# Sixty instead of forty-four seven-product quads in a two-layer encoder's MLPs, with residual additions by accumulating DMA

## The chip, the core and the metric

The kernel runs on one core of one Trainium2 chip. The metric is the device time of one execution in microseconds. The core's engines are TensorE (PE; its weight loads are listed as PEld), VectorE (DVE), ScalarE (ACT), GpSimd (POOL) and SyncE (SP, which here only issues DMAs). Each engine works through its own queue in order.

## The reference

256 tokens of width 2048 pass through two layers. Layer 0 mixes tokens with a convolution module, layer 1 with latent attention; each is followed by an MLP of width 8192, whose two products are most of the work. Everything is float32.

```python
def sq_relu_mlp(h, w1, w2):
    return jnp.square(jax.nn.relu(h @ w1)) @ w2

# for each layer
x = x + mixer(rms_norm(x, norm_mixer_g[i]))
x = x + sq_relu_mlp(rms_norm(x, norm_mlp_g[i]), mlp_w1[i], mlp_w2[i])
# at the end
return rms_norm(x, final_norm_g)
```

## The kernel before

The residual `xs` stays on chip: 128 partitions, two token tiles (t = 0, 1), 2048 columns, which are four blocks of 512 (n = 0 to 3). A float32 product is made of three products of rounded parts: `mm3` adds hi x hi, lo x hi and hi x lo. The weights stream in by DMA from SP's queue, 1 MB at a time, into `raw` (three buffers). ACT makes the `hi` part (L168, for mixed quads L489) and DVE the `lo` part by a subtraction (L172, for mixed quads L490); `hi` and `lo` have six buffers each (`WB`).

**The MLP** runs in two halves of the 8192 columns; (layer, half) names one of the four half-layers. The up product of a half goes through eight groups g of 512 columns (L615, L616). After a group's last matmul DVE and ACT evacuate it (L634 to L643): square of the positive part, then hi and lo for the next product. The down product follows. It takes two column blocks at a time, a pair, and walks over the half's 32 k-tiles in 16 **quads** of 2 k-tiles x 2 blocks x 2 token tiles.

**Plain and mixed quads.** A plain quad is 8 `mm3`, so 24 matmuls of 128x512. A mixed quad computes the same 2x2 block product with seven multiplications instead of eight: 21 matmuls. For this it needs sums of the four weight blocks, made by DVE in `raw` (L497, L498, L499) before their hi and lo parts, and sums of the inputs, made in the evacuation of its group (`mixed_inputs`). The table `MIXED` says which groups of each half-layer are mixed; each is two mixed quads in each of two column pairs.

**The sums.** `Sums` holds the eight PSUM banks of a pair: four `e[t][c]`, into which plain quads go straight, and four `u`, which only the mixed quads feed and from which three of the four outputs need combinations. `join` makes these after the last mixed quad and adds them to `xs`: one ACT copy and eight DVE operations (L568 to L575). At the pair's end `add` (L376) adds the `e` banks to `xs` with four DVE operations.

**The order** is that of the program's text on each engine. In a pair the quads alternate, mixed ahead of plain, until the mixed ones are used up. In the second pair of a second half, `product_A` takes the place of the plain quads: it goes through the plain groups with one block of 24 matmuls each for n = 2 (4 k-tiles x 2 token tiles), with mixed quads between, and then through n = 3.

**The two ends.** In layer 0's last half the finished residual must be turned (columns to partitions) for the next mixer. Blocks 0 to 2 are turned by DVE: `turn_block` issues 48 STREAM_TRANSPOSE (L322), spread by `turns_on` between the quads of the last column pair, and ACT and DVE then make hi and lo parts. Block 3 is turned by `to_T` with TensorE (L265). In layer 1's last half ACT sums the squares of each finished block (L399) and DVE multiplies it by the final gain (L1769).

The profile's names: `sh`, `sl` are input parts of mixed groups, `gh`, `gl` of plain ones.

Of the kernel before, what the change touches and what calls it, by code (L numbers as in the profile page):

```python
# [21 lines left out]
T = 2  # L22
# [13 lines left out]
HALVES = 2  # L36
PAD_CONST = 24
PAD_SMALL = 48
# [39 lines left out]
def trunk_kernel(  # L78
# [324 lines left out]
    def product_A(  # L403
# [14 lines left out]
        for n in blocks:  # L418
# [54 lines left out]
        while due:  # L473
            prepare(due.pop(0))

    def turns_on(due, prepare, n=4):

        if due and not steps:
            prepare(due.pop(0))
        step(n)  # L480

# [41 lines left out]
    class Sums:  # L523
# [36 lines left out]

        def join(self, pool):

            u1, u6, u7, u5 = self.u
            x = lambda t, c: xs[:, t, (self.n + c) * NB : (self.n + c + 1) * NB]
            a, b = (pool.tile([P, 2, S], F32, tag="v", name=nm("v"), bufs=2).rearrange("p a n -> p (a n)") for _ in range(2))
            tt = nc.vector.tensor_tensor
# [3 lines left out]
            tt(b, u7, a, op=ALU.add)  # L570
            tt(a, u5, a, op=ALU.add)
            tt(x(1, 0), b, x(1, 0), op=ALU.add)
            tt(b, u5, b, op=ALU.add)
            tt(x(0, 1), a, x(0, 1), op=ALU.add)
            tt(x(1, 1), b, x(1, 1), op=ALU.add)  # L575

    def mlp(layer, ssq, next_gain, finish=None, before=None, beside=None):

        with ExitStack() as cx:
# [3 lines left out]
            nssq = None  # L583
            turned = None if next_gain is None else mp.tile([P, NB // P, S], F32, name=nm("turned"))
            r2_row = mp.tile([P, S], F32, name=nm("r2_row"))
            repool(f"mlp{layer}", acc=8)

            def scales():
# [8 lines left out]
            for hf in range(HALVES):  # L597
# [4 lines left out]
                for g in range(ng):  # L602
# [20 lines left out]
                    if g in mixed or len(mixed) < N_MIXED and g == plain[-1]:  # L623
                        shape = [P, 2, 7, P] if g in mixed else [P, 4, S]
                        gs[g] = [mp.tile(shape, F32R, tag=f"s{c}", name=nm(f"s{c}"), bufs=N_MIXED) for c in "hl"]
                    else:
                        gs[g] = [mp.tile([P, 4, S], F32R, tag=f"g{c}", name=nm(f"g{c}"), bufs=ng - N_MIXED) for c in "hl"]
                    gh, gl = gs[g]
                    for b2 in range(2):
                        v = mp.tile([P, 2, S], F32, tag="v", name=nm("v"), bufs=2)  # L630
                        for b in range(2):
# [11 lines left out]
                        nc.vector.tensor_tensor(gl[:, bs, :], v, gh[:, bs, :].bitcast(F32), op=ALU.subtract)  # L643
                nssq, add, prepare = residual_stage(
                    last, next_gain, None, turned, () if turned is None else range(NNB - 1)
                )
                w, k_lo = mlp_w2[layer], hf * nkh
# [9 lines left out]
                for n in range(0, NNB - 2 * last, 2):  # L657
                    sums = Sums(n)
                    ks = [4 * g + 2 * b for g in plain for b in range(2)]
                    for i, k in enumerate(ks):  # L660
                        if i < len(ms):
                            mixed_quad(sums, i)
                            turns_on(due, prepare)
                        if i == len(ks) - 2:
                            sums.join(mp)
                        sums.plain(w, k_lo + k, hi, lo, k, i == len(ks) - 1)
                        turns_on(due, prepare)
                    for c in range(2):
                        for t in range(T):
                            add(n + c, [sums.e[i][c] for i in range(T)], t)  # L670
                        if last:
                            due.append(n + c)
                if last:
# [3 lines left out]
                    def between(n, u, due):  # L677
                        if n == n2 and u < len(plain) - 1:
                            lo_i, hi_i = (len(ms) * i // (len(plain) - 1) for i in (u, u + 1))
                            for i in range(lo_i, hi_i):  # L680
                                mixed_quad(sums, i)
                                turns_on(due, prepare)
                        if n == n2 and u == len(plain) - 1:
                            sums.join(mp)

                    product_A(
                        w, k_lo, nkh, hi, lo, add, prepare, range(n2, NNB), due,
# [8 lines left out]
    with ExitStack() as cx:  # L696
# [3 lines left out]
        NW = W * KC // 4  # L700
        w_dw = const.tile([P, W * KC], F32, name="w_dw")

# [543 lines left out]
    def rotary_tables(pool):  # L1246

        place = pool.tile([P, 2, S], F32, tag="v", name=nm("v"), bufs=2).rearrange("p a n -> p (a n)")
        at = [0]
# [512 lines left out]

    with tc.tile_pool(name="fin", bufs=1, reuse_waits="tile") as fp:
        gf = fp.tile([P, D], F32, name="gf")
        nc.scalar.dma_start(gf, final_norm_g.rearrange("(a n) -> a n", a=1).partition_broadcast(P))

        def gained(t, n):
            sl = slice(n * NB, (n + 1) * NB)
            nc.vector.tensor_tensor(xs[:, t, sl], xs[:, t, sl], gf[:, sl], op=ALU.mult)  # L1769

        def finish(ssq, t):
# [18 lines left out]
            for i, (c0, c1) in enumerate(zip(cuts, cuts[1:])):  # L1790
                ob = xs[:, t, c0:c1]
                if c1 == D:
                    nc.vector.scalar_tensor_tensor(
                        out=ob, in0=ob, scalar=y, in1=gf[:, c0:c1], op0=ALU.mult, op1=ALU.mult
                    )
# [24 lines left out]

        mlp(1, ssq, None, finish, before)

# [25 lines left out]
```

## Time and profile before

| | us |
|---|---|
| median of three timed runs | 1955.56 |
| lowest and highest | 1955.26, 1955.60 |
| profiled execution, its own time | 1955.42 |
| profiled span | 1953.6 |
| PE busy | 1932.2 |
| DVE busy | 1547.1 |
| ACT busy | 1058.6 |
| POOL busy | 220.5 |

A row of a group reads: line, engine, operation, output <- input, shapes, count | busy us, mean ns of one | idle us just before them, and what ended it. A row of waits reads: engine, line, what it waited for, us in total, how often, the longest. In a timeline a row begins with its start and its duration in us, "x2" is two instructions in a row, and a bracket at the end gives the idle time before it. In a table of windows each row gives the window, its length, and each engine's busy time; then the granted clock, the DMA engines' busy share and their GB/s. The last number of a DMA row is the time in us from issue to landing. A matmul's busy time overlaps with the next one's.

The down products of the four half-layers, as windows in the trace (first matmul of the pair to that of the next): (0,0) 477.85 to 560.82 and 560.82 to 643.78; (0,1) 821.29 to 905.63 and 905.63 to 996.52; (1,0) 1435.41 to 1518.39 and 1518.39 to 1601.35; (1,1) 1778.86 to 1861.84 and 1861.84 to 1944.00, after which the output is finished.

### The profile page before, as it was taken

The numbers are of one execution on the slowest core, as the hardware profiler recorded it, in microseconds if no ns is written. First come the engines' busy times: TensorE is split into PE (matmuls) and PEld (weight loads), VectorE is DVE, ScalarE is ACT, GpSimd is POOL, SyncE is SP. The second block draws the span as 40 slices with busy tenths as digits, with TensorE's granted clock in tenths as the row PEclk, the third lists the DMA queues.
The fourth block names the chain that finished last, engine by engine and source line by source line (L and its number), as shares of the span: only waits on it lengthen the run. The fifth ranks groups of instructions, "written<-read, shape, count | busy, mean of one in ns | idle before, by whom it ended". The sixth has DMA issues, their size and how long they took to land. (4 is left out here: it accounts for less than half of the span.)

```text
span 1953.6 us, 28331 instructions
## 1 busy us (share of the span) xinstructions
PE 1932.2 (99%) x10835; PEld 1691.2 (87%) x10835; DVE 1547.1 (79%) x2400; ACT 1058.6 (54%) x1568; POOL 220.5 (11%) x172
## 2 busy tenths in 40 slices
PE   8999999999999999999999999999999999999998
PEld 8999888888888888888789998888888888888886
DVE  7999988877988676787966665876788876778896
ACT  5667755554645454454556665555555545455554
POOL 6999100000000000000001310000000000000000
PEclk9999999999999999999999999999999999999999
DMA  7765556664657666564565445566656566664754
GB/s 231 209 192 175 169 180 212 194 187 159 225 191 231 191 185 188 169 231 157 172 193 173 120 144 180 173 223 189 192 171 217 193 222 190 193 193 160 237 168 147
DMA packets 216746, 367.62 MB, mean 188 GB/s; under 512 B 15513, under 2 KB 90529, under 8 KB 216353
## 3 DMA queue, kind: packets, MB, share of 16 engines
q1 hardware_dynamic: 215280, 363.28, 58.7%
q10 hardware_dynamic: 1328, 2.52, 0.4%
q8 instruction: 85, 1.39, 0.3%
q14 instruction: 53, 0.43, 0.1%
HBM read 363.68 MB, written 2.10 MB: 187 GB/s over the span
## 5 line engine op out<-in xcount | busy, mean ns | idle before, releaser
L172 DVE TENSOR_TENSOR lo<-raw,hi 128x1024 fp32r<-128x1024 f32 (+2 forms) x543 | 647.9, 1205 | 294.7 <-ACT hi L168 290.8
L168 ACT ACTIVATE hi<-raw 128x1024 fp32r<-128x1024 f32 (+2 forms) x608 | 622.8, 1040 | 462.6 <-PE acc L615 238.7
L615 PE MATMUL acc<-xt,hi 128*128 128x512 f32 x2048 | 710.5, 390 | 0.0
L616 PE MATMUL acc<-xt,lo 128*128 128x256 f32 x2048 | 577.5, 282 | 0.0
L615 PEld LDWEIGHTS acc<-xt,hi 128*128 128x128 f32 x2048 | 384.4, 188 | 80.6
L616 PEld LDWEIGHTS acc<-xt,lo 128*128 128x128 f32 x2048 | 387.1, 189 | 0.2
L489 ACT ACTIVATE hi<-raw 128x1024 fp32r<-128x1024 f32 (+1 forms) x176 | 164.0, 949 | 179.8 <-DVE raw L497 70.1
L203 PE MATMUL acc<-lo,gh 128*128 128x512 f32 (+1 forms) x644 | 250.2, 388 | 1.1 <-DVE lo L172 0.9
L201 PE MATMUL acc<-hi,gh 128*128 128x512 f32 (+1 forms) x644 | 249.7, 388 | 0.0
L202 PE MATMUL acc<-hi,gl 128*128 128x512 f32 (+1 forms) x644 | 249.7, 388 | 0.0
L490 DVE TENSOR_TENSOR lo<-raw,hi 128x1024 fp32r<-128x1024 f32 (+1 forms) x176 | 188.5, 1087 | 34.2 <-ACT hi L489 30.6
L761 PE MATMUL acc<-xt,hi 128*128 128x256 f32 x1024 | 180.1, 281 | 0.3 <-ACT b L1043 0.2
L848 DVE SCALAR_TENSOR_TENSOR sum<-ub,w_dw,sum 128x256 f32<-128x256 f32 x409 | 164.2, 480 | 3.5 <-ACT sum L818 3.0
L203 PE MATMUL acc<-lo,sh 128*128 128x512 f32 x404 | 157.8, 391 | 2.8 <-DVE lo L490 2.6
L201 PE MATMUL acc<-hi,sh 128*128 128x512 f32 x404 | 157.4, 390 | 0.0
L172 POOL TENSOR_TENSOR lo<-raw,hi 128x1024 fp32r<-128x1024 f32 x65 | 154.9, 2408 | 17.3 <-ACT hi L168 17.3
L761 PEld LDWEIGHTS acc<-xt,hi 128*128 128x128 f32 x1024 | 154.6, 188 | 1.1 <-ACT xt L1027 0.6
L203 PEld LDWEIGHTS acc<-lo,gh 128*128 128x128 f32 x644 | 120.9, 188 | 27.5 <-DVE lo L172 2.7
L201 PEld LDWEIGHTS acc<-hi,gh 128*128 128x128 f32 x644 | 120.9, 188 | 24.8
L202 PEld LDWEIGHTS acc<-hi,gl 128*128 128x128 f32 x644 | 120.9, 188 | 24.7
L761 PE MATMUL acc<-xt,lo 128*128 128x256 f32 x512 | 139.2, 279 | 0.0
L202 PE MATMUL acc<-hi,sl 128*128 128x512 f32 x340 | 132.4, 389 | 0.0
(310 smaller groups left out, 2359.5 us busy)
## 6 DMA issues: line engine op xcount, KB each, us to landing
raw<-in_mlp_w SPq DMA_DIRECT2D x256, 1024.0 KB, 5.4
raw<-in_conv_w_pw SPq DMA_DIRECT2D x62, 512.0 KB, 5.1
raw<-in_conv_w_pw SPq DMA_DIRECT2D x16, 1024.0 KB, 5.1
raw<-in_mla_w_o SPq DMA_DIRECT2D x16, 1024.0 KB, 5.6
raw<-in_mla_w_kv_up SPq DMA_DIRECT2D x8, 1024.0 KB, 5.5
raw<-in_mla_w_in SPq DMA_DIRECT2D x8, 576.0 KB, 3.7
raw<-in_mla_w_in SPq DMA_DIRECT2D x4, 1024.0 KB
raw<-in_mla_w_q_up SPq DMA_DIRECT2D x16, 256.0 KB, 3.3
```

The source lines that it names most:

```text
L168: nc.scalar.activation(hi, raw[:, js, :], AF.Copy)
L172: eng.tensor_tensor(lo, raw, hi.bitcast(F32), op=ALU.subtract)
L201: nc.tensor.matmul(ps, sh, mh, start=start, stop=False)
L202: nc.tensor.matmul(ps, sl, mh, start=False, stop=False)
L203: nc.tensor.matmul(ps, sh, ml, start=False, stop=stop)
L489: nc.scalar.activation(hi, src, AF.Copy)
L490: nc.vector.tensor_tensor(lo, src, hi.bitcast(F32), op=ALU.subtract)
L615: nc.tensor.matmul(ps[b], wh[:, bs], xhl(k), start=k == 0, stop=False)
L616: nc.tensor.matmul(ps[b][:, :S], wl[:, bs], xh(k), start=False, stop=k == KC - 1)
L761: nc.tensor.matmul(pss[c][b][:, :S], w[i][:, bs], (xh, xl)[j](k), start=k == i + j == 0, stop=end and k == k0 + nk - 1 and (i, j) == terms ...
L848: nc.vector.scalar_tensor_tensor(out=out, in0=ubs[c][:, w : w + S], scalar=tap(c, w), in1=base, op0=ALU.mult, op1=ALU.add)
```

## The change

Four things are changed.

1. `MIXED` grows from 11 to 15 groups: 60 mixed quads instead of 44, four groups in each half-layer but (0,1), which has three. The order in a pair follows a rule with `TAIL`: for eight mixed (m) and eight plain (p) quads it is m m p m p m p m m p m p m p p p. In (0,1) it is m p m p m p p m p m p m p p p p. In the second pair of a second half `between` is now called ahead of the first block too; with G for a block of 24 matmuls, (0,1) runs m G m G m G m G m m G and (1,1) m m G four times.
2. `join` makes its combinations in four tiles (`v`, four buffers instead of two), one ACT copy and four DVE operations, and POOL issues four accumulating DMAs (`put`, 256 KB each, SBUF to SBUF) that add them to `xs`. `close` takes the place of `add` where a pair runs over quads: DVE adds block 0, and for block 1 ACT copies each bank to a tile and a `put` adds it. That is 44 DMAs: 8 joins x 4 and 6 closes x 2.
3. In layer 0's last half blocks 0 to 2 are turned by TensorE as well: `prepare` runs `to_T` after the first, second and third group of n = 3. 48 STREAM_TRANSPOSE go, 24 transposes of 128x128 come, and the tile `turned` goes.
4. Room: `w_dw` moves to another pool, one padding shrinks, and the final gain `gf` is loaded later (`after_up`).

```diff
-MIXED = {(0, 0): (0, 2, 4), (0, 1): (0, 2), (1, 0): (0, 2, 4), (1, 1): (0, 2, 4)}
-N_MIXED = 3
+MIXED = {(0, 0): (0, 2, 4, 6), (0, 1): (0, 2, 4), (1, 0): (0, 2, 4, 6), (1, 1): (0, 2, 4, 6)}
+N_MIXED = 4
+TAIL = 3
...
             for u, g in enumerate(groups):
+                if u == 0 and beside is not None:
+                    beside(n, -1, due)
...
-                else:
-                    turns_on(due, prepare)
+                elif n == blocks[-1]:
+                    for _ in range(len(due) if n_end else min(1, len(due))):
+                        prepare(due.pop(0))
...
+        def put(self, t, c, o):
+            nc.gpsimd.dma_start(self.place(t, c), o, accum_op=ALU.add)
+
+        def join(self, room):
             u1, u6, u7, u5 = self.u
-            a, b = (pool.tile([P, 2, S], F32, tag="v", name=nm("v"), bufs=2).rearrange("p a n -> p (a n)") for _ in range(2))
+            a, b, c, d = (room() for _ in range(4))
             nc.scalar.activation(a, u1, AF.Copy)
-            tt(x(0, 0), u1, x(0, 0), op=ALU.add)
-            tt(a, u6, a, op=ALU.add)
...
+            nc.vector.tensor_tensor(b, u6, a, op=ALU.add)
+            nc.vector.tensor_tensor(c, u7, b, op=ALU.add)
+            nc.vector.tensor_tensor(d, u5, c, op=ALU.add)
+            nc.vector.tensor_tensor(b, u5, b, op=ALU.add)
+            for (t, n), o in (((0, 0), a), ((1, 0), c), ((1, 1), d), ((0, 1), b)):
+                self.put(t, n, o)
+
+        def close(self, room):
+            for c in range(2):
+                for t in range(T):
+                    e, x = self.e[t][c], self.place(t, c)
+                    if c == 0:
+                        nc.vector.tensor_tensor(x, e, x, op=ALU.add)
+                    else:
+                        o = room()
+                        nc.scalar.activation(o, e, AF.Copy)
+                        self.put(t, c, o)
...
+                    at = 0
                     for i, k in enumerate(ks):
-                        if i < len(ms):
-                            mixed_quad(sums, i)
-                            turns_on(due, prepare)
+                        upto = -(-len(ms) * (i + 1) // (len(ks) - TAIL + 1))
+                        while at < min(upto, len(ms)):
+                            mixed_quad(sums, at)
+                            at += 1
                         if i == len(ks) - 2:
-                            sums.join(mp)
+                            sums.join(room)
                         sums.plain(w, k_lo + k, hi, lo, k, i == len(ks) - 1)
-                        turns_on(due, prepare)
-                    for c in range(2):
-                        for t in range(T):
-                            add(n + c, [sums.e[i][c] for i in range(T)], t)
+                    sums.close(room)
...
-                        if n == n2 and u < len(plain) - 1:
-                            lo_i, hi_i = (len(ms) * i // (len(plain) - 1) for i in (u, u + 1))
+                            lo_i, hi_i = (len(ms) * i // len(plain) for i in (u + 1, u + 2))
```

In the changed kernel L488 is what L490 was, L173 what L172 was, L495 to L497 what L497 to L499 were, L651 to L660 the evacuation, and L1787 the gain.

The first place is DVE's queue at the start of the down product of (0,0), before. `raw_710` is the first plain quad's, `raw_715` the second mixed quad's; `acc_665` to `acc_668` are the banks of the last up group.

```order
L172 TENSOR_TENSOR lo_712_5490<-raw_710_5487,hi_711_5489 128x1024
L634 TENSOR_TENSOR v_691_5419<-acc_665_5245,v_691_5419 128x256
L634 TENSOR_TENSOR v_691_5419<-acc_666_5246,v_691_5419 128x256
L634 TENSOR_TENSOR v_692_5428<-acc_667_5247,v_692_5428 128x256
L635 SCALAR_TENSOR_TENSOR v_691_5419<-v_691_5419 128x512
L172 TENSOR_TENSOR lo_714_5494<-raw_710_5487,hi_713_5493 128x1024
L637 TENSOR_TENSOR v_691_5419<-v_691_5419,r2_row_460_3772 128x512
L634 TENSOR_TENSOR v_692_5428<-acc_668_5248,v_692_5428 128x256
L490 TENSOR_TENSOR lo_717_5524<-raw_715_5521,hi_716_5523 128x1024
L643 TENSOR_TENSOR gl_690_5418<-v_691_5419,gh_689_5417 128x512
L635 SCALAR_TENSOR_TENSOR v_692_5428<-v_692_5428 128x512
L490 TENSOR_TENSOR lo_719_5528<-raw_715_5521,hi_718_5527 128x512
```

The same place after the change: `raw_709` is the second mixed quad's.

```order
L488 TENSOR_TENSOR lo_711_5505<-raw_709_5502,hi_710_5504 128x1024
L651 TENSOR_TENSOR v_690_5434<-acc_664_5260,v_690_5434 128x256
L651 TENSOR_TENSOR v_690_5434<-acc_665_5261,v_690_5434 128x256
L651 TENSOR_TENSOR v_691_5443<-acc_666_5262,v_691_5443 128x256
L652 SCALAR_TENSOR_TENSOR v_690_5434<-v_690_5434 128x512
L651 TENSOR_TENSOR v_691_5443<-acc_667_5263,v_691_5443 128x256
L654 TENSOR_TENSOR v_690_5434<-v_690_5434,r2_row_459_3771 128x512
L652 SCALAR_TENSOR_TENSOR v_691_5443<-v_691_5443 128x512
L488 TENSOR_TENSOR lo_713_5509<-raw_709_5502,hi_712_5508 128x512
L660 TENSOR_TENSOR gl_689_5433<-v_690_5434,gh_688_5432 128x512
L654 TENSOR_TENSOR v_691_5443<-v_691_5443,r2_row_459_3771 128x512
L495 TENSOR_TENSOR raw_709_5502<-raw_709_5502 128x1024
```

The two lo parts of the plain quad (L172) have left this stretch, since that quad now comes later. The second mixed quad's first lo stands ahead of the evacuation and its other parts in the evacuation, three rows earlier than before.

The second place is DVE's queue in the last pair but one block of layer 0, n = 2 in (0,1), before: a mixed quad, with turning between its parts, and the first lo's of a block of 24.

```order
L490 TENSOR_TENSOR lo_1316_9186<-raw_1312_9179,hi_1315_9185 128x512
L497 TENSOR_TENSOR raw_1312_9179<-raw_1312_9179 128x1024
L322 STREAM_TRANSPOSE turned_459_3771<-xs_85 32x2x4x32
L498 TENSOR_TENSOR raw_1312_9179<-raw_1312_9179 128x512
L322 STREAM_TRANSPOSE turned_459_3771<-xs_85 32x2x4x32
L499 TENSOR_TENSOR raw_1312_9179<-raw_1312_9179 128x512
L490 TENSOR_TENSOR lo_1318_9193<-raw_1312_9179,hi_1317_9192 128x1024
L322 STREAM_TRANSPOSE turned_459_3771<-xs_85 32x2x4x32
L490 TENSOR_TENSOR lo_1320_9197<-raw_1312_9179,hi_1319_9196 128x1024
L322 STREAM_TRANSPOSE turned_459_3771<-xs_85 32x2x4x32
L172 TENSOR_TENSOR lo_1323_9228<-raw_1321_9225,hi_1322_9227 128x1024
L172 TENSOR_TENSOR lo_1325_9232<-raw_1321_9225,hi_1324_9231 128x1024
```

After the change, a mixed quad and a block of 24 of the same pair, and the next mixed quad's beginning:

```order
L488 TENSOR_TENSOR lo_1325_9095<-raw_1323_9092,hi_1324_9094 128x1024
L488 TENSOR_TENSOR lo_1327_9099<-raw_1323_9092,hi_1326_9098 128x512
L495 TENSOR_TENSOR raw_1323_9092<-raw_1323_9092 128x1024
L496 TENSOR_TENSOR raw_1323_9092<-raw_1323_9092 128x512
L497 TENSOR_TENSOR raw_1323_9092<-raw_1323_9092 128x512
L488 TENSOR_TENSOR lo_1329_9106<-raw_1323_9092,hi_1328_9105 128x1024
L488 TENSOR_TENSOR lo_1331_9110<-raw_1323_9092,hi_1330_9109 128x1024
L173 TENSOR_TENSOR lo_1334_9137<-raw_1332_9134,hi_1333_9136 128x1024
L173 TENSOR_TENSOR lo_1336_9141<-raw_1332_9134,hi_1335_9140 128x1024
L488 TENSOR_TENSOR lo_1339_9171<-raw_1337_9168,hi_1338_9170 128x1024
L488 TENSOR_TENSOR lo_1341_9175<-raw_1337_9168,hi_1340_9174 128x512
L495 TENSOR_TENSOR raw_1337_9168<-raw_1337_9168 128x1024
```

The transposes are gone from between the parts of the mixed quad, and nothing stands in their place on DVE.

The third place is DVE's queue where the second pair of (1,1) begins, before: the first mixed quad (`raw_2698`) of that pair, with the four additions of the closed pair and the gains.

```order
L490 TENSOR_TENSOR lo_2702_17607<-raw_2698_17600,hi_2701_17606 128x512
L498 TENSOR_TENSOR raw_2698_17600<-raw_2698_17600 128x512
L376 TENSOR_TENSOR xs_85<-acc_2575_16945,xs_85 128x512
L499 TENSOR_TENSOR raw_2698_17600<-raw_2698_17600 128x512
L376 TENSOR_TENSOR xs_85<-acc_2577_16947,xs_85 128x512
L1769 TENSOR_TENSOR xs_85<-xs_85,gf_12488 128x512
L376 TENSOR_TENSOR xs_85<-acc_2576_16946,xs_85 128x512
L1769 TENSOR_TENSOR xs_85<-xs_85,gf_12488 128x512
L376 TENSOR_TENSOR xs_85<-acc_2578_16948,xs_85 128x512
L490 TENSOR_TENSOR lo_2704_17614<-raw_2698_17600,hi_2703_17613 128x1024
L490 TENSOR_TENSOR lo_2706_17618<-raw_2698_17600,hi_2705_17617 128x1024
L1769 TENSOR_TENSOR xs_85<-xs_85,gf_12488 128x512
```

After the change: `raw_2789` is the second mixed quad's. The first L1787 row is block 0 of both token tiles, the other two are block 1, whose additions are `put`s.

```order
L583 TENSOR_TENSOR xs_85<-acc_2650_17113,xs_85 128x512
L583 TENSOR_TENSOR xs_85<-acc_2652_17115,xs_85 128x512
L1787 TENSOR_TENSOR xs_85<-xs_85,gf_17758 128x512 x2
L488 TENSOR_TENSOR lo_2791_17805<-raw_2789_17802,hi_2790_17804 128x1024
L488 TENSOR_TENSOR lo_2793_17809<-raw_2789_17802,hi_2792_17808 128x512
L495 TENSOR_TENSOR raw_2789_17802<-raw_2789_17802 128x1024
L1787 TENSOR_TENSOR xs_85<-xs_85,gf_17758 128x512
L496 TENSOR_TENSOR raw_2789_17802<-raw_2789_17802 128x512
L488 TENSOR_TENSOR lo_2795_17816<-raw_2789_17802,hi_2794_17815 128x1024
L497 TENSOR_TENSOR raw_2789_17802<-raw_2789_17802 128x512
L1787 TENSOR_TENSOR xs_85<-xs_85,gf_17758 128x512
L488 TENSOR_TENSOR lo_2797_17820<-raw_2789_17802,hi_2796_17819 128x1024
```

Two of the four additions have left DVE. The gains of block 1 stand between the sums and the last two lo parts of the second mixed quad, and each follows the landing of a transfer.

More of the change, by code (lines that the diff above doesn't have):

```diff
@@ L622, in mlp @@
                         beside = None
-                    if g in mixed or len(mixed) < N_MIXED and g == plain[-1]:
+                    if g in mixed or g in plain[len(plain) + len(mixed) - N_MIXED :]:
                         shape = [P, 2, 7, P] if g in mixed else [P, 4, S]
@@ L643, in mlp @@
                         nc.vector.tensor_tensor(gl[:, bs, :], v, gh[:, bs, :].bitcast(F32), op=ALU.subtract)
-                nssq, add, prepare = residual_stage(
-                    last, next_gain, None, turned, () if turned is None else range(NNB - 1)
-                )
+                nssq, add, prepare = residual_stage(last, next_gain)
                 w, k_lo = mlp_w2[layer], hf * nkh
@@ L1246, in rotary_tables @@
     def rotary_tables(pool):
[L1248 removed]
+        place = pool.tile([P, 2, S], F32, tag="v", name=nm("v"), bufs=4).rearrange("p a n -> p (a n)")
         at = [0]
@@ L1819, in before @@
                     gained(t, n)
-        mlp(1, ssq, None, finish, before)
+        mlp(1, ssq, None, finish, before, after_up=load_gf)
 _INS = [
```

49 lines of the change are left out of this document (22 added, 27 removed).

## The prediction

> **What bounds the kernel now.** I read the page first: the span, the engines' busy shares, the slices of the span (busy share in tenths), and the chain that ended last.
>
> ```profile
> span 1953.6 us, 28331 instructions
> ...
> PE 1932.2 (99%) x10835; PEld 1691.2 (87%) x10835; DVE 1547.1 (79%) x2400; ACT 1058.6 (54%) x1568; POOL 220.5 (11%) x172
> ...
> PE   8999999999999999999999999999999999999998
> ...
> DVE  7999988877988676787966665876788876778896
> ...
> PEclk9999999999999999999999999999999999999999
> ...
> PE 47%; ACT 1%; DVE 1%; POOL 0%; issue 0%; DVEq 0%; ACTq 0%
> ```
>
> The profiled execution took 1955.42 us, 0.14 us below the median of the three timed runs (1955.56), so a sum against the one holds for the other. PE works in every slice at full clock, and the chain runs through PE matmuls. So only two things shorten the kernel: fewer matmuls, or a stretch in which PE stands still. I therefore cut the span into the stages of the MLP's down product, which the change rewrites, with the last up groups of the first half-layer ahead of them.
>
> ```profile
> core 0: us, PE busy (x) PEld busy (x) DVE busy (x) ACT busy (x) POOL busy (x), PEclk, DMA share, GB/s
> 400.00:477.85 77.85, 77.85 (x452) 69.00 (x451) 53.91 (x75) 37.81 (x53) 0.00 (x0) 1.00 0.57 177
> ...
> 477.85:560.82 82.97, 82.97 (x368) 68.70 (x367) 73.44 (x82) 43.90 (x49) 0.00 (x0) 1.00 0.61 203
> ...
> 821.29:905.63 84.34, 84.34 (x375) 69.85 (x373) 64.28 (x72) 42.79 (x49) 0.00 (x0) 1.00 0.65 213
> 905.63:996.52 90.89, 87.05 (x373) 68.87 (x371) 85.16 (x123) 44.95 (x63) 0.18 (x2) 1.00 0.51 165
> ...
> 1778.86:1861.84 82.98, 82.98 (x369) 68.70 (x368) 74.06 (x84) 45.25 (x53) 0.00 (x0) 1.00 0.62 209
> ```
>
> A column pair with three mixed groups has 6 quads of 21 and 10 of 24 matmuls: 366, in 82.97 us, or 0.2267 us each. Half-layer (0,1) has two mixed groups: 4 x 21 + 12 x 24 = 372, in 84.34 us, again 0.2267. Its second pair (905.63 to 996.52) has the same 372 but takes 90.89 us: 6.55 us are lost there. It is the only down stage where DVE is nearly full (85.16). The waits of that stretch, PE's and its weight load's, say on what:
>
> ```profile
> PE acc L203 <- DVE lo L490: 2.6, 2, 1.6
> PE acc L203 <- DVE lo L172: 0.9, 1, 0.9
> PEld acc L203 <- DVE lo L490: 4.4, 4, 2.0
> PEld acc L203 <- DVE lo L172: 3.2, 5, 1.3
> ```
>
> PE waits there for the low parts of weights that DVE makes. Elsewhere DVE is ahead, but by little: one cycle of a mixed and a plain quad reads so on DVE.
>
> ```profile
> 502.63 1.81 DVE L490 TENSOR_TENSOR lo<-raw,hi 128x1024 fp32r<-128x1024 f32 x2
> 504.37 1.22 DVE L497 TENSOR_TENSOR raw<-raw 128x1024 f32<-128x1024 f32 x1
> 505.62 0.69 DVE L498 TENSOR_TENSOR raw<-raw 128x512 f32<-128x512 f32 x1
> 506.34 0.69 DVE L499 TENSOR_TENSOR raw<-raw 128x512 f32<-128x512 f32 x1
> 506.95 2.52 DVE L490 TENSOR_TENSOR lo<-raw,hi 128x1024 fp32r<-128x1024 f32 x2
> 509.39 2.35 DVE L172 TENSOR_TENSOR lo<-raw,hi 128x1024 fp32r<-128x1024 f32 x2
> 511.66 1.82 DVE L490 TENSOR_TENSOR lo<-raw,hi 128x1024 fp32r<-128x1024 f32 x2
> ```
>
> The mixed quad takes DVE from 502.63 to 509.39, 6.76 us, and the plain one 2.27 to 511.66. PE needs 21 x 0.2267 = 4.76 for the first and 24 x 0.2267 = 5.44 for the second. Mixed plus plain is 9.03 on DVE against 10.20 on PE: covered. Two mixed and one plain are 15.79 against 14.96: DVE loses 0.83 each time. A mixed quad is cheaper for PE and too dear for DVE alone.
>
> **The change part by part.**
>
> *Sixteen more mixed quads.* 16 x 3 = 48 matmuls go. At the 0.2267 us that a matmul adds to a full stretch this is **-10.9**. The group's own duration would say otherwise:
>
> ```profile
> L203 PE MATMUL acc<-lo,gh 128*128 128x512 f32 (+1 forms) x644 | 250.2, 388 | 1.1 <-DVE lo L172 0.9
> ...
> L322 DVE STREAM_TRANSPOSE turned<-xs 32x256 f32<-32x256 f32 x48 | 20.9, 436 | 1.0
> ```
>
> 48 x 388 ns would be -18.6. I take the stage rate, since 366 x 0.388 = 142 us does not fit into 82.97. The Trainium skill, "Trainium Kernel Development and Optimization", Performance Expectations, agrees: it calls matmul busy time a bad metric because matmuls are pipelined, and this trace shows 0.388 against 0.2267. The inputs' extra sums fall into the up product; DVE has 77.85 - 53.91 = 23.9 us free in its last stretch. Without that cover they would cost what the g7 evacuation costs below.
>
> *The first layer's end.* 48 STREAM_TRANSPOSE, 20.9 us of DVE, leave the stage 905.63 to 996.52. 85.16 less these is 64.3; two mixed quads in the place of plain ones add 2 x (6.76 - 2.27) = 9.0: 73.3, as in the stages at 477.85 and 1778.86, which PE works through without a loss. The order there becomes one mixed quad and one block of 24 matmuls, 9.03 against 10.20, with one double near the end. So the waits go; 0.3 of the 6.55 I leave at the end, where the last block is still turned: **-6.2** (bounds -6.55 and 0). What comes instead are 24 transposes on PE among the last block's matmuls.
>
> ```profile
> 1057.67 0.87 PE tr L265 x8
> ```
>
> Eight take 0.87 us where they stand in a row, 0.109 each; 24 of them **+2.6**. Each wants its bank and residual done some 10 us before, so I add no wait.
>
> *The order at the three starts from up to down.* In (0,0), (1,0) and (1,1) the order is now mixed, mixed, plain. The second mixed quad follows at 477.85 + 21 x 0.2267 = 482.61 instead of 5.44 later. DVE at that time still evacuates the last up group:
>
> ```profile
> 477.48 1.12 DVE L634 TENSOR_TENSOR v<-acc,v 128x256 f32<-128x256 f32 x3
> ...
> 479.12 1.22 DVE L172 TENSOR_TENSOR lo<-raw,hi 128x1024 fp32r<-128x1024 f32 x1
> ...
> 481.20 1.21 DVE L490 TENSOR_TENSOR lo<-raw,hi 128x1024 fp32r<-128x1024 f32 x1
> ...
> 490.18 1.23 DVE L490 TENSOR_TENSOR lo<-raw,hi 128x1024 fp32r<-128x1024 f32 x1 [1.21 <-ACT hi L489]
> ```
>
> The chain from 477.48 ends at 491.41. In the new order one plain lo (1.15 from start to start) is behind it and the first mixed lo (1.14) ahead of it, so the quad's last lo is ready at about 489.1. The matmul that wants it is the 18th of the quad, at 482.61 + 17 x 0.2267 = 486.5. PE waits **2.5** us at each start, **+7.5** in all (bounds 0 and 3 x 5). The idle 1.21 ahead of the last lo stays: ACT makes hi from a sum that DVE finishes just before. (0,1) still begins mixed, plain, mixed: 0. After the start the plain quads of the tail give the lead back. The second pairs of (0,0) and (1,0) begin with two mixed quads too, behind DVE's two additions but without an evacuation, and I see about 1 us of margin: 0, bound 2 x 2.5.
>
> *Additions by DMA.* 44 transfers of 256 KB on a queue that had none. Before shows no accumulating transfer; the nearest rows are plain ones of that size:
>
> ```profile
> raw<-in_mlp_w SPq DMA_DIRECT2D x256, 1024.0 KB, 5.4
> ...
> raw<-in_mla_w_q_up SPq DMA_DIRECT2D x16, 256.0 KB, 3.3
> ...
> out<-xs SPq DMA_DIRECT2D x5, 256.0 KB, 3.6
> ```
>
> I take 3.6 us, the row that also starts at the residual, with 3.3 below and, since adding means a second read and weights move beside it, 8 above. The Trainium skill, "DMA: Bandwidth & Descriptors", Anatomy of one DMA, fits 2.0 us + bytes / 436e3 for this path, an estimate of 2.6 us; no run here shows it, and the sum by it would be 1.0 lower. The load is 11.5 MB in a DMA share of 0.5 to 0.65: hidden. So are DVE's saved additions, as DVE is not the end there. What counts is who waits for a landing. In (0,0), (1,0) the next reader comes at the next close, two quads (10.9 us) after the join: 0 up to that landing time. In (1,1) it comes at once: the gains L1787 of block 1 stand in DVE's queue between the parts of the second mixed quad. When block 1's sums are ready, and how long a copy by ACT of that size takes, is seen here:
>
> ```profile
> 559.66 0.69 DVE L376 TENSOR_TENSOR xs<-acc,xs 128x512 f32<-128x512 f32 x1 [0.67 <-PE acc L203]
> 561.02 0.69 DVE L376 TENSOR_TENSOR xs<-acc,xs 128x512 f32<-128x512 f32 x1 [0.67 <-PE acc L203]
> ```
>
> ```profile
> L399 ACT ACTIVATE scratch<-xs 128x512 f32<-128x512 f32 (+1 forms) x32 | 19.8, 620 | 17.3 <-DVE xs L376 16.8
> ```
>
> In this pair, the first of (0,0), which ends at 560.82, the first of the two is read 1.16 before the end and the other 0.2 after it. With the copy (0.62) and 3.6 the first has landed 3.1 after the end. From there DVE has, in the order of its queue, a gain (0.68), a sum (0.69), a lo (1.22), a sum, the other gain and a lo: up to 8.3, where PE wants the last at 4.76 + 3.85 = 8.6. Two plain lo's and two mixed quads bring DVE to 8.3 + 2.27 + 2 x 6.76 = 24.1; PE wants that at 14.96 + 8.6 = 23.6, so it waits 0.5 to 0.6, and the two cycles that follow add 0.83 each. Together **+2.3**; with a landing at 5 us +3.7, at 8 us +6.7. At the very end the last additions wait for a join's transfer that starts a group earlier: **+0.3** (0 to 0.6; 3 at 8 us).
>
> Sum: -10.9 - 6.2 + 2.6 + 7.5 + 2.3 + 0.3 = -4.4, so 1955.4 - 4.4 = **1951.0 us**.
>
> **The rivals.**
>
> *DVE keeps up at the starts.* If scheduling lets the evacuation finish sooner, the 7.5 go and the sum is -11.9: 1943.5; without the 2.3 too, 1941.2. For it: DVE idles 23.9 us in the stretch before. Against it: the chain hangs on the last up matmul, before which nothing can be evacuated. Half of it gone gives 1947.3.
>
> *Transfers land late: slower.* Accumulating transfers at 8 us or more turn waits of DVE, whose queue is in order, into PE's: at 8 us 4.4 + 2.7 more, sum +2.7, 1958.1. Each us beyond adds one at (1,1)'s second pair and one at the end: 9 us give 1960.1, 10 us 1962.1; it is slower by my bound from about 8.6 us. Over 10.9 us the 6 closes wait as well. For it: the addition is a read more than any row of before shows, and the weights' 1 MB loads hold half to two thirds of the same DMA engines. Against it: 256 KB at 3.3 to 3.6 us under such loads. DVE is 85 to 90% busy in these stages. A rule would bring this about: the Trainium skill, "SBUF — State Buffer", SBUF: two separate sides, says that DVE in a two-port mode locks GpSimd out of writing descriptors, so that its transfers sit waiting; no run here shows it.
>
> *DVE becomes the bound inside the mixed stretches.* If its lead is never rebuilt, each doubled pair costs 0.83 in every stage: (0,0), (1,0) have two doubles in each of two pairs, (1,1) two in its first: 10 x 0.83 = 8.3, of which the starts hold 2.5 already. The other seven are +5.8: 1956.8. Against it: the tail, three plain quads in a row at 2.27 against 5.44, rebuilds 9 us.
>
> That the change does not do what it says I give nothing: the order shows 5792 matmuls of 512 columns.
>
> **How the numbers follow.** A measurement of this kernel can tell about 0.2%, 3.9 us, from no change; faster begins below 1951.6. The forecast case has 0.43; its spread (starts 2 to 3 us each, landing 3.3 to 5) is 1949.2 to 1953.9, and half of it lies below the bound: 0.22 faster, 0.21 same. DVE keeps up, wholly or by half: 0.26, faster. Late transfers: 0.19, slower in 0.16 and same in 0.03. DVE the bound: 0.12, same in 0.10, and slower in 0.02 where a late landing joins it. Faster 0.48, same 0.34, slower 0.18. The range leaves out the rival without any wait (1941.2) and landings over 9 us: **1943 to 1960**.
>
> **What would show it.** Down stages (0,0) first pair: 8 x 21 + 8 x 24 = 360 matmuls, 81.6 us plus 2.5, with PE waiting on L488's lo some 8 us after the start; second pair 81.6. The second pair of (0,1), now 366 matmuls, 83.0 + 2.6, without waits. (1,1) second pair with ACT or DVE waiting on a DMA right after the close. The DMA row of L563 near 3.6 us. It would be wrong if PE shows no gap at the starts (1943.5), if transfers take 8 us and DVE waits on them (1958 and up), or if the (0,1) stage keeps its 6 us.

## The result, and the profile after

| us | before | after |
|---|---|---|
| median of twelve timed runs | 1955.52 | 1952.89 |
| lowest and highest | 1955.26, 1955.79 | 1950.55, 1955.17 |
| profiled execution, its own time | 1955.42 | 1954.63 |
| profiled span | 1953.6 | 1952.8 |

The ratio is 0.9986, with a 95% interval of 0.9978 to 0.9995: 2.6 us faster, where 4.4 were forecast. The changed kernel's times lie 4.6 us apart, those of before 0.5. The profiled execution is the second slowest of the twelve, 1.7 us above their median. What follows is read from it.

The page after, its engines and its slices of PE:

```profile
span 1952.8 us, 28589 instructions
...
PE 1926.6 (99%) x10811; PEld 1683.5 (86%) x10811; DVE 1574.7 (81%) x2436; ACT 1090.9 (56%) x1628; POOL 259.2 (13%) x216
...
PE   8999999999999999999999999999999999999997
```

The page would let one think that nothing is left to ask: PE at 99%, as before. The stages tell more. These windows are the pairs of (0,0), of (0,1) and of (1,1); columns as in the prediction.

```profile
477.97:561.60 83.63, 82.52 (x363) 67.26 (x361) 78.29 (x87) 46.62 (x54) 3.65 (x4) 1.00 0.65 208
561.60:643.20 81.60, 81.60 (x362) 67.57 (x360) 73.42 (x75) 46.03 (x51) 5.22 (x6) 1.00 0.74 232
820.71:903.68 82.97, 82.97 (x368) 68.73 (x367) 70.49 (x77) 45.63 (x54) 3.58 (x5) 1.00 0.67 215
903.68:989.36 85.68, 85.68 (x391) 71.01 (x389) 69.33 (x79) 49.24 (x68) 5.33 (x8) 1.00 0.68 207
1769.28:1852.78 83.50, 82.20 (x362) 67.33 (x361) 78.78 (x88) 47.01 (x57) 3.50 (x4) 1.00 0.70 222
1852.78:1944.68 91.90, 84.88 (x372) 67.22 (x371) 75.70 (x92) 47.44 (x63) 5.25 (x6) 1.00 0.58 176
```

Where no wait is, 360 matmuls take 81.60 us and 366 take 82.97: six fewer save 1.37. The first pairs of (0,0) and (1,1) lose 2.0 and 1.9 at their starts. The second pair of (0,1), which took 90.89, takes 85.68 with its 24 transposes. The second pair of (1,1) should take 81.6 and takes 91.90: over 10 us are lost in a stage that lost nothing before, when its 366 matmuls read so:

```profile
1861.84:1944.82 82.98, 82.98 (x378) 69.18 (x377) 69.95 (x87) 42.92 (x56) 0.00 (x0) 1.00 0.50 165
```

From a half-layer's first down matmul to the next up product, the spans changed by -0.70 in (0,0), -8.30 in (0,1) with the mixer behind it, -0.71 in (1,0) and +8.79 in (1,1) with the kernel's end; the up products did not change.

In that last pair the waits of PE name three things, and the DMA row says how late the transfers are:

```profile
PE acc L204 <- DVE lo L173: 3.2, 2, 2.3
PE acc L202 <- ACT hi L487: 2.4, 4, 1.3
PE acc L204 <- DVE lo L488: 1.3, 2, 0.8
```

```profile
xs<-v POOLq DMA_DIRECT2D x44, 256.0 KB, 7.2
```

7.2 us is the median from issue to landing; the 44 lie between 3.2 and 10.1. ACT's timeline at the start of the pair shows what such a landing does:

```profile
1852.68 0.58 ACT L586 ACTIVATE v<-acc 128x512 f32<-128x512 f32 x1
1853.16 1.05 ACT L487 ACTIVATE hi<-raw 128x1024 fp32r<-128x1024 f32 x1
1854.11 0.59 ACT L586 ACTIVATE v<-acc 128x512 f32<-128x512 f32 x1
1854.59 0.63 ACT L487 ACTIVATE hi<-raw 128x512 fp32r<-128x512 f32 x1
1859.32 0.63 ACT L400 ACTIVATE scratch<-xs 128x512 f32<-128x512 f32 x1 [4.10 <-DMA xs<-v]
1859.86 0.19 ACT L400 ACTIVATION_READ_ACCUMULATOR scratch<-xs 128x1 f32 x1
1859.95 1.04 ACT L487 ACTIVATE hi<-raw 128x1024 fp32r<-128x1024 f32 x1
```

The two copies (L586) are what the transfers move, and GpSimd issues both only after the second has begun:

```profile
1854.52 1.76 POOL L563 DMA_DIRECT2D xs<-v  x2 [9.04 <-ACT hi L487]
```

ACT then stands 4.1 us with the squares of block 1 at the head of its queue, and the hi part that PE needs is behind them. At the pair's end it is DVE, with a lo part behind the addition:

```profile
1919.72 0.68 DVE L377 TENSOR_TENSOR xs<-acc,xs 128x512 f32<-128x512 f32 x1
1925.51 0.69 DVE L377 TENSOR_TENSOR xs<-acc,xs 128x512 f32<-128x512 f32 x1 [5.11 <-DMA xs<-v]
1926.11 1.21 DVE L173 TENSOR_TENSOR lo<-raw,hi 128x1024 fp32r<-128x1024 f32 x1
```

Added up from the starts of the matmuls, PE lost 4.3 us in the pair's first 14 us, 2.0 in the three cycles that follow, and 3.7 at the end, 1924.7 to 1930: 10.0 in all.

### The profile page after: what moved, and what is told of

The parts are those of the page before. It is cut to its first block, busy times and chain, and to the rows that moved or that the text cites. A ratio compares the mean times of both kernels' runs of the same rounds, so it can differ in the third digit from the quotient of the medians.

```text
span 1952.8 us, 28589 instructions
## 1 busy us (share of the span) xinstructions
PE 1926.6 (99%) x10811; PEld 1683.5 (86%) x10811; DVE 1574.7 (81%) x2436; ACT 1090.9 (56%) x1628; POOL 259.2 (13%) x216
## 4 chain that ended last, share of the span: by engine, by line
PE 66%; issue 25%; DVE 4%; DMA 3%; ACT 1%; POOL 1%; SPq 0%; DVEq 0%; ACTq 0%; POOLq 0%
PE acc L632 18%; PE acc L633 9%; PE acc L202 9%; PE acc L204 9%; PE acc L203 8%; PE acc L776 8%; PE acc L1239 2%; DMA xs<-v 2%; DVE sum L863 1%; DVE lo L173 1%; POOL xs L563 1%; DVE lo L488 0%; DMA xs<-in_x 0%; ACT hi L169 0%; PE acc L1623 0%
## 5 line engine op out<-in xcount | busy, mean ns | idle before, releaser
L173 DVE TENSOR_TENSOR lo<-raw,hi 128x1024 fp32r<-128x1024 f32 (+2 forms) x511 | 607.7, 1204 | 262.1 <-ACT hi L169 256.7
L487 ACT ACTIVATE hi<-raw 128x1024 fp32r<-128x1024 f32 x240 | 222.5, 948 | 221.7 <-DVE raw L495 123.6
L488 DVE TENSOR_TENSOR lo<-raw,hi 128x1024 fp32r<-128x1024 f32 x240 | 256.1, 1087 | 33.3 <-ACT hi L487 29.3
L202 PE MATMUL acc<-hi,sh 128*128 128x512 f32 x516 | 202.3, 392 | 5.6 <-ACT hi L487 5.4
L204 PE MATMUL acc<-lo,gh 128*128 128x512 f32 (+1 forms) x516 | 199.7, 388 | 3.2 <-DVE lo L173 3.2
L204 PE MATMUL acc<-lo,sh 128*128 128x512 f32 x516 | 199.5, 390 | 1.7 <-DVE lo L488 1.6
L202 PE MATMUL acc<-hi,gh 128*128 128x512 f32 (+1 forms) x516 | 200.3, 388 | 0.0
L203 PE MATMUL acc<-hi,gl 128*128 128x512 f32 (+1 forms) x516 | 200.0, 388 | 0.0
L203 PE MATMUL acc<-hi,sl 128*128 128x512 f32 x452 | 176.0, 389 | 0.0
L173 POOL TENSOR_TENSOR lo<-raw,hi 128x1024 fp32r<-128x1024 f32 x65 | 154.9, 2406 | 17.3 <-ACT hi L169 17.3
L202 PEld LDWEIGHTS acc<-hi,sh 128*128 128x128 f32 x516 | 96.9, 188 | 30.2 <-ACT hi L487 10.7
```

The source lines that it names most:

```text
L173: eng.tensor_tensor(lo, raw, hi.bitcast(F32), op=ALU.subtract)
L202: nc.tensor.matmul(ps, sh, mh, start=start, stop=False)
L203: nc.tensor.matmul(ps, sl, mh, start=False, stop=False)
L204: nc.tensor.matmul(ps, sh, ml, start=False, stop=stop)
L487: nc.scalar.activation(hi, src, AF.Copy)
L488: nc.vector.tensor_tensor(lo, src, hi.bitcast(F32), op=ALU.subtract)
```

## The experiments

The theory after this reading: the late landings in (1,1) cost 8 us, the starts 5.7, and both are apart from the matmuls' gain. Times of before, taken with each set of experiments, have medians of 1955.15 to 1955.49. Ratios are to these, each with its 95% interval.

**1. Without any transfer.** `join` and `close` use DVE as before, the rest is as changed.

```diff
-            for (t, n), o in (((0, 0), a), ((1, 0), c), ((1, 1), d), ((0, 1), b)):
-                self.put(t, n, o)
+            # join: the eight DVE operations of before
...
-                    if c == 0:
+                    if c == 0 or self.by_dve:
```

> The changed kernel with all 44 accumulating transfers taken out: DVE makes the joins and closes as before, everything else as changed. Theory (late landings in (1,1)): of the 10 us that PE stands still in the second pair of (1,1), the start (4.3) and the end (3.8) go, and the DVE additions give back 1 to 2 us at the starts of second pairs; 1945 to 1947 us, and the timed runs lie within 1 us of each other as before. Rival (DVE is too full in that pair whatever adds): the stall stays or grows, 1953 or more.

Measured 1949.58 (1948.86 to 1950.21), ratio 0.9971 [0.9959, 0.9982]: 3.3 faster than the changed kernel, not 6 to 8. Between the two profiled executions the gain is all in (1,1): 183.57 to 178.39 from its first down matmul to the end. That is 5.2, more than between the medians, since the profiled execution of the changed kernel was one of its slow ones. The spans of the other half-layers are the same to 0.02 us, so DVE's additions cost nothing there, nor do transfers. But in the second pair of (1,1) 4.9 us of standing still remain, and DVE and ACT parts are what PE waits for:

```profile
PE acc L202 <- ACT hi L487: 2.0, 6, 0.6
PE acc L204 <- DVE lo L488: 0.5, 1, 0.5
```

So theory and rival are both half right: the transfers cost about half of the 10 us. The other half stays whatever adds. My reading is that the order mixed, mixed, block is too much for DVE, and for the hi parts that ACT makes of DVE's sums; experiment 9 tests it.

**2. Transfers everywhere but in (1,1).** The flag of the first experiment, for the last half of layer 1 alone (`last and layer == 1`).

> Transfers only where the next reader is a pair away: DVE adds in the last half of layer 1 alone, transfers elsewhere. Theory: as much faster as without any transfer, or 1 us more, 1944 to 1946 us, with little spread. Rival (the transfers' traffic slows the weights' loads everywhere): little is won here, 1950 to 1952, while the kernel without any transfer is clearly faster than this one.

Measured 1949.66 (1949.27 to 1950.67), ratio 0.9972 [0.9961, 0.9982]: as without any transfer. 34 of the 44 transfers are left, and what they move costs nothing; the loss is where the next reader is near. The level was off as in the first experiment, for the same reason.

**3. No pair that runs over quads starts with two mixed ones.** The second pair of (1,1), which runs over blocks, keeps its order m m G, though the expectation speaks of every pair.

```diff
                         upto = -(-len(ms) * (i + 1) // (len(ks) - TAIL + 1))
+                        if len(ms) == len(ks):
+                            upto = (1, 2, 3, 5, 6, 8, 8, 8)[i]
```

> The changed kernel with another order of a pair's eight mixed and eight plain quads: m p m p m p m m p m p m m p p p, so that no pair starts with two mixed quads. Theory: the waits of 1.9 us at the three starts from up to down go, 5.7 us: 1947 us. Rival (the wait only moves to the doubled quads, as DVE's lead is short there too): 1952 to 1953.

Measured 1949.41 (1948.57 to 1952.64), ratio 0.9973 [0.9962, 0.9984]. Between the medians it gains 3.5, between theory and rival. The waits at the starts did go: the spans of (0,0) and (1,0) fall from 165.23 to 163.21 each, 2.0 as expected, with no gap left. In (1,1), 183.57 becomes 181.33 in the profiled execution, the fastest of the eight; PE still stands still for 9.6 us in its second pair. The spread of these runs, 4.1 us, is nearly that of the changed kernel, and in experiments 1 and 2, which have no transfers in (1,1), it is 1.4. So the spread probably comes from there, which one trace can't show.

**4. The turning alone.** 44 mixed quads in the old order and DVE's additions, with TensorE's transposes.

```diff
-MIXED = {(0, 0): (0, 2, 4, 6), (0, 1): (0, 2, 4), (1, 0): (0, 2, 4, 6), (1, 1): (0, 2, 4, 6)}
+MIXED = {(0, 0): (0, 2, 4), (0, 1): (0, 2), (1, 0): (0, 2, 4), (1, 1): (0, 2, 4)}
...
-                        upto = -(-len(ms) * (i + 1) // (len(ks) - TAIL + 1))
+                        upto = i + 1
```

> The turning by TensorE alone: 44 mixed quads in the order of before and additions by DVE. Theory: DVE's 20.9 us of transposes leave the second pair of (0,1), PE's 6.2 us of waits there and 1.3 to 1.7 just behind it go, 24 transposes cost 2.6: 1950.0 to 1950.5 us. Rival (the waits go only because DVE's additions went as well): 1953 or more.

Measured 1951.14 (1950.96 to 1951.35), ratio 0.9978 [0.997, 0.9987]. From the first down matmul of (0,1) to the next layer's up product 436.38 becomes 432.58: -3.8, against -6.2 + 2.6 = -3.6 in the prediction. The time is 0.6 above the expected range. The wait of 1.3 just behind the turning stayed here, and it is gone with 60 quads. Why is not settled; it is the only part of (0,1) that the prediction's terms don't hold. This one edit is worth more than the whole change, 4.1 us against 2.6: the 16 quads with their order and the transfers together gave back 1.5. Of the 4.1, 0.7 are not the turning's: the last output's transfer lands after 3.35 us instead of 4.01, in this kernel as in the changed one (3.37).

**5. Plain copies.** `accum_op` is left out of `put`, so the additions by DMA are not made and the residual is overwritten.

> The changed kernel with the 44 transfers as plain copies (accumulation left out, so the residual is overwritten): what of the median 7.2 us to landing is the addition. Theory (the addition's second read and write make them late): 3.5 to 4.5 us, near the plain transfers of that size. Rival (GpSimd's issue and the weights' loads beside them make them late): 6 to 7 us, hardly less, and the time stays at 1952 to 1953.

One profiled execution: 5.1 us median instead of 7.2, 2.2 to 8.7, and (1,1) at 178.54 as without transfers; 1949.9 in one run. The landing falls between the two expectations: the addition accounts for 2 of the 7.2 us, and the rest is there for a plain copy too. The time did not stay at 1952 to 1953, as the rival had it, but one run can't tell more.

```profile
xs<-v POOLq DMA_DIRECT2D x44, 256.0 KB, 5.1
```

**6. GpSimd makes lo parts.** DVE's additions, the order of experiment 3, and GpSimd subtracts for the n = 2 blocks of 24 in (1,1).

```diff
-    def load_split(srcs, nj):
-        return split(load(srcs, nj), nc.vector)
+    def load_split(srcs, nj, eng=None):
+        return split(load(srcs, nj), eng or nc.vector)
```

> All additions by DVE, the order m p m p m p m m p m p m m p p p, and in the second pair of (1,1) GpSimd makes the lo parts of the four blocks of 24 matmuls of n = 2, eight subtractions, in DVE's place. Theory (DVE is the bound of that pair, 15.8 against 14.96 a cycle): DVE has 13.5 a cycle, the waits of 0.97, 1.07 and 1.24 go and the start loses under 1.6; 1939 to 1941 us. Rival (GpSimd is too slow for it or holds DVE up): 1943.5 or more, with PE waiting on GpSimd's lo or on DVE as before.

Measured 1953.12 (1952.88 to 1954.65), ratio 0.9989 [0.998, 0.9997]: 7 us slower than the same kernel without it (experiment 7). The rival held. PE waits for GpSimd's parts:

```profile
PE acc L204 <- POOL lo L173: 5.2, 7, 1.4
```

And GpSimd holds DVE up. The timeline of GpSimd, and DVE's at the first such block:

```profile
1858.01 5.28 POOL L173 TENSOR_TENSOR lo<-raw,hi 128x1024 fp32r<-128x1024 f32 x2 [723.90 <-ACT hi L169]
...
1876.52 5.80 POOL L173 TENSOR_TENSOR lo<-raw,hi 128x1024 fp32r<-128x1024 f32 x2 [13.23 <-PE acc L204]
```

```profile
1855.15 0.68 DVE L497 TENSOR_TENSOR raw<-raw 128x512 f32<-128x512 f32 x1
...
1858.16 2.87 DVE L1802 TENSOR_TENSOR xs<-xs,gf 128x512 f32<-128x512 f32 x1
1860.95 4.02 DVE L488 TENSOR_TENSOR lo<-raw,hi 128x1024 fp32r<-128x1024 f32 x2
```

A DVE gain of 0.68 us takes 2.87 and a pair of lo's that takes 1.82 elsewhere takes 4.02, while GpSimd's two subtractions run. Both begin while GpSimd is at work and are longer by 2.2 us, nearly one of its subtractions. Those suffer too: 2.4 us each in the first layer of before, up to 3.38 here. The two engines took turns.

**7. DVE's additions and the order of experiment 3, nothing else.**

> All additions by DVE and the order m p m p m p m m p m p m m p p p, nothing else. Theory (the two add up): 1949.6 - 6.1 = 1943.5 us. Rival (without the waits at the starts the stall turns up behind the closes, where DVE adds more than with transfers): 1945 to 1947.

Measured 1946.02 (1945.85 to 1946.65), ratio 0.9952 [0.9939, 0.9964]. The rival's range held it: (0,0) and (1,0) keep the 2.0 us that each gained, but (1,1) goes from 178.39 to 179.03 although its first pair is 1.9 shorter. PE comes to the second pair earlier, but by the pair's second cycle DVE is where it was, 110.2 us after the half-layer's first down matmul in both kernels. The stall there grows from 4.9 to 7.4 us: the rival's mechanism, in one place.

**8. 64 mixed quads.** As experiment 6, also for (0,1), with a fourth mixed group there.

```diff
-(0, 1): (0, 2, 4),
+(0, 1): (0, 2, 4, 6),
```

> As the kernel with GpSimd's lo parts, also in (0,1), and with a fourth mixed group there: 64 mixed quads. Theory (PE is the bound wherever DVE has room): 12 matmuls less, 2.7 us less than that kernel, 1936.5 to 1938.5. Rival (the pairs of (0,1) become DVE's as those of (1,1) were): no gain or a loss of 2 us against that kernel.

Measured 1961.76 (1961.61 to 1962.0), ratio 1.0032 [1.002, 1.0044]. (0,1) with the mixer takes 436.69 instead of 428.08. That is 8.6 us more than experiment 6, worse than either expectation. It holds two changes at once, and since experiment 6 showed that GpSimd's share is itself a loss, it does not tell what the fourth group alone would do.

**9. Three mixed groups in the last half.** Experiment 7 with 56 quads:

```diff
-(1, 1): (0, 2, 4, 6)}
+(1, 1): (0, 2, 4)}
```

> All additions by DVE, the order m p m p m p m m p m p m m p p p where a half-layer has four mixed groups, and three mixed groups instead of four in the last half of layer 1 (56 mixed quads), whose pairs then have the order of (0,1). Theory (two mixed quads to a block of 24 are more than DVE can serve, one is not): 12 matmuls more, 2.7 us, against the 7.3 us that PE stood still in that second pair: 1946.0 + 2.7 - 7.3 = 1941.4 us. Rival (the stall comes from the closing of the pair, gains and squares in the queues, not from the count): 1946 to 1949.

Measured 1941.31 (1941.17 to 1941.42), ratio 0.9929 [0.9915, 0.9943]; 1941.4 was expected. PE has no gap left in (1,1). The windows of its two pairs:

```profile
1765.52:1848.49 82.97, 82.97 (x368) 68.72 (x367) 74.72 (x84) 45.24 (x53) 0.00 (x0) 1.00 0.64 215
1848.49:1931.48 82.99, 82.99 (x378) 69.21 (x377) 69.75 (x87) 42.94 (x56) 0.00 (x0) 1.00 0.50 171
```

DVE is busy for 69.75 of 82.99 us in the second, against 75.70 of 91.90 in the changed kernel: twelve matmuls more in the two pairs are cheaper than the waits. One mixed group less also brings the order m G in the place of m m G, and the run does not tell the two apart.

**10. The same with the transfers.** Experiment 9, with all 44 transfers as changed.

> The same with the 44 transfers of the changed kernel in the place of DVE's additions. Theory (late landings are paid where the next reader follows at once): at the start of the last pair ACT's squares and DVE's gains wait some 6 us for a landing, of which one mixed quad and a block of 24 cover a part, and at the end PE waits 3.8 as in the changed kernel; 4 to 7 us over the kernel with DVE's additions, 1945.5 to 1948.5. Rival (landings hurt only where DVE is full): within 1.5 us of it.

Measured 1941.18 (1940.98 to 1941.57), ratio 0.9929 [0.9916, 0.9942]: the rival held, the theory of late landings fell. The transfers land as late as before (7.8 median), and DVE waits for one even longer at the end:

```profile
1903.94 0.68 DVE L377 TENSOR_TENSOR xs<-acc,xs 128x512 f32<-128x512 f32 x1
1910.22 0.69 DVE L377 TENSOR_TENSOR xs<-acc,xs 128x512 f32<-128x512 f32 x1 [5.60 <-DMA xs<-v]
1910.83 1.22 DVE L173 TENSOR_TENSOR lo<-raw,hi 128x1024 fp32r<-128x1024 f32 x1
```

PE has no gap there: it works on blocks whose lo parts DVE had made before the wait. Two things gave it these, which the run does not tell apart, one block of 24 more at the end (five plain groups instead of four) and the lead from one mixed quad to a block. At the pair's start the two transfers landed after 3.4 and 3.5 us, for a reason that I have not found, and ACT waited 0.4 instead of 4.1, so that place is no test. The late landing at the end was not a price by itself: it was paid where the order and the count had left no lead.

## Why the prediction was right or wrong

*The time.* 1952.9 lies in the range, 1.9 above the forecast, and within 0.2% of before, which had 0.34. The step that was mis-sized is the term of the additions in (1,1). That the sum came so near is in part luck: in the profiled execution, 3.6 above the forecast, this term and that of the end missed by 7.4, and the starts and the turning by 3.4 the other way.

*The matmuls, -10.9.* Right: 81.60 us for 360 and 82.97 for 366, 0.2267 each. The mean duration's -18.6 would have been wrong.

*The first layer's end, -6.2 + 2.6.* Right: -3.8 alone in experiment 4. PE's timeline shows a turn of one block:

```profile
964.66 0.39 PE L204 MATMUL acc<-lo,gh 128*128 128x512 f32 x1
964.89 1.03 PE L266 MATMUL acc<-ident,xs 128*128 128x128 f32 x8
965.68 0.48 PE L202 MATMUL acc<-hi,gh 128*128 128x512 f32 x1
```

From 964.89 to 965.68 are 0.79 us, and 0.09 is lost in the next matmul: 0.88 a block, 2.6 for three. Another 1.7 went just behind, which I had not seen in the trace of before: the next mixer's first matmuls lost 1.25 and 0.2 us there, the first of them waiting for DVE.

*The starts, +7.5.* Right in place, too large: 1.9 to 2.0 each, 5.8. (The prediction's own 489.1 and 486.5 leave 2.6 for the wait, not the 2.5 it used.) DVE's timeline ends the chain when it was forecast to, 487.96 + 1.23 = 489.2 against 489.1:

```profile
482.53 1.22 DVE L495 TENSOR_TENSOR raw<-raw 128x1024 f32<-128x1024 f32 x1
...
486.09 0.68 DVE L497 TENSOR_TENSOR raw<-raw 128x512 f32<-128x512 f32 x1
487.96 1.23 DVE L488 TENSOR_TENSOR lo<-raw,hi 128x1024 fp32r<-128x1024 f32 x1 [1.18 <-ACT hi L487]
```

```profile
486.23 0.73 PE L204 MATMUL acc<-lo,sh 128*128 128x512 f32 x2
487.98 0.50 PE L202 MATMUL acc<-hi,sh 128*128 128x512 f32 x1 [1.02 <-ACT hi L487]
488.31 0.40 PE L203 MATMUL acc<-hi,sl 128*128 128x512 f32 x1
```

But PE's row of waits is on ACT's hi, and four products with that hi come ahead of the first with the lo: the matmul that wants the lo is the 20th of the quad, not the 18th. I had taken the order of `mm3` for PE's order.

*The additions, +2.3 and +0.3.* Wrong: 6.3 and 3.7. The cause in the prediction's terms: the landing of 3.6 us was 7.2 in the middle of all, 4.7 and 5.4 at the close in (1,1) and up to 9.4 at the end; and DVE's queue was counted but not ACT's. ACT's queue counts twice. The prediction had the first transfer issued 0.5 us before the pair's end and landed 3.1 after it. It was issued 1.7 after the end (1854.52 against 1852.78), since ACT's copies stand behind the squares of block 0 and a hi part, and landed 6.5 after: 2.3 of the 3.4 us are the later issue and 1.1 the landing. And behind the copies the squares of block 1 hold up the next hi part by 4.1 us.

The sizes of 3.3 and 3.6 were the lower rows of that size. The trace of before also had these, at the program's start with the DMA engines at a share of 0.95 to 0.99, and the prediction left them out:

```profile
raw<-in_conv_w_pw SPq DMA_DIRECT2D x4, 256.0 KB, 8.2
...
xs<-in_x SPq DMA_DIRECT2D x2, 256.0 KB, 7.3
```

The rival of late transfers had this mechanism, which at 8 us gave 7.1 more; 7.4 more were measured. That the numbers agree is chance: the landings at the close were not 8 us, and experiment 1 shows that half of the 10 us stays without any transfer. There four mixed groups with their order m m G are the likely cause, which I had priced within the 2.3. The time stayed below that rival's 1958 since 1.7 at the starts and 1.7 behind the turning came back. And experiment 10 shows that DVE's wait for a landing costs nothing where PE is supplied.

*DVE as the bound.* Outside (1,1)'s second pair it did not happen: 81.60 in the second pair of (0,0) with two doubled quads. Inside, the forecast of 0.83 for a cycle is 0.4 to 0.8 in the changed kernel and 0.8 to 1.25 in experiment 1.

*Not seen at all:* that the time would scatter over 4.6 us. Where PE meets DVE with a margin the runs agree: 0.25 apart in experiment 9, 0.6 in experiment 10 with the same transfers.

## What to carry to other kernels

A cheaper form of a product that moves work from the full engine to the next one pays only up to the ratio that this one can serve, stage by stage: 56 quads in a looser order, with the same transfers, were 11.7 us faster here than the 60 of the change. A lead, the finished parts that an engine holds ready for PE, is spent once: at a stage's start and where two heavy steps follow each other, look for the engine that has no lead, and count the queues of all engines in their own order, not in the order of the source. Before pricing a slow transfer, ask whether its reader has other work queued behind it that somebody will miss.

## What the runs showed of the hardware

Accumulating transfers of 256 KB from SBUF to SBUF landed 7.2 us after their issue in the median, plain ones from the same queue 5.1 (experiment 5). Plain ones from SP landed after 3.0 to 3.6 in the median, but after 7.3 to 8.2 at the program's start. GpSimd needs 0.87 us to issue an accumulating one and 0.54 a plain one. The shortest landing was 3.2 us, and DVE was busy for all but 0.04 us of it (window of that transfer); the longest ones, of over 9 us, fall where the DMA engines are nearly full (a share of 0.85 or more) and another is on its way. The first row is the shortest, the second a long one, the third a short one beside full engines, so that a full share alone does not make a transfer late:

```profile
1909.91:1913.11 3.20, 2.92 (x12) 1.91 (x11) 3.16 (x4) 3.11 (x4) 0.86 (x1) 1.00 0.64 154
1844.32:1853.88 9.56, 9.56 (x44) 7.92 (x43) 8.78 (x11) 4.67 (x8) 1.17 (x2) 1.00 0.99 236
903.59:907.06 3.47, 3.47 (x17) 2.88 (x16) 2.69 (x3) 3.04 (x4) 1.72 (x2) 1.00 1.03 274
```

That DVE at work starves these transfers, the rule weighed in the prediction, is not what the first row shows. It remains open for DVE forms that do not occur here.

DVE and GpSimd do block each other when both run subtractions or products of SBUF tiles: 0.68 became 2.87 us on DVE and 2.4 up to 3.38 on GpSimd in experiment 6. The Trainium skill, "SBUF — State Buffer", SBUF: two separate sides, says this of a DVE operation with two inputs there against a GpSimd operation that reads there: whichever starts first holds a shared port for its whole duration. The trace agrees: the multiply that began 0.15 us after GpSimd's first subtraction (1858.01 to 1860.48) ended 0.55 after it.
